# A two-layer decoder trunk on one core: eight-tile inversion on array quarters, S5's loads on another queue, eleven dummy products

## The chip, the cores and the metric

The kernel runs on one core of one Trainium2 chip. The metric is the device time of one execution in microseconds (us); the time before is the median of three runs. A profile is one execution recorded by the hardware profiler. TensorE is called PE, VectorE DVE, ScalarE ACT, GpSimd POOL, SyncE SP.

## What is computed

The reference is a decoder trunk of two layers over 1024 positions of width 1024, in float32. Layer 0 mixes positions by a gated DeltaNet (GDN, 8 heads of 128, chunks of 64 positions), layer 1 by a diagonal state-space model (S5, 64 groups of 16 channels). Beside each mixer runs a cross-attention into 256 memory tokens; an output projection, a layer norm, an MLP and another layer norm follow. Cut to what matters here:

```
a_strict = where(strict, einsum('bhnid,bhnjd->bhnij', kb, k) * decay, 0)
sol = triangular_solve(eye + a_strict, concat([vb, kb * exp(gc)]))    # per head and chunk
...                                                                   # scan over chunks with sol
st = sr + pr * h - pi * h ...                                         # S5: complex scan, chunk by chunk
y = Re(C st) + D u
x = LN(alpha * x + concat([mix, cross]) @ w_o);  x = LN(alpha * x + relu(x @ w1)**2 @ w2)
```

The kernel works in chunks of 128 positions, eight tiles a head, and inverts each tile's unit lower triangular 128x128 matrix (eye + a_strict) instead of solving with it.

## The kernel before, in words

**Large products.** The matrices of the projections and the MLP are split into a high and a low part of type fp32r, and three products replace one (`mm3`, lines 380 to 385; wi, wz, wu, q and so on in the profile). ACT makes the high part (L362, L851), DVE the low part (L363, L852). Small products (recurrence, inversion, S5's tables) are plain fp32, which PE runs as two instructions each.

**The GDN part.** For each head, `gdn_projections` makes keys, queries, values and the gate. `gdn_keys_out` writes the negated strictly lower matrices of a half (four tiles) to DRAM as ntf, and their diagonal blocks of 32 as ntd. `gdn_inverse_` inverts the blocks of 32 on DVE for two heads at a time and leaves them in DRAM as t32, once as they are and once transposed. `gdn_invert_tiles` then puts the blocks together: first from 32 to 64, then from 64 to the tile's 128. Before, this runs by halves of a head: four tiles at a time, five steps, each a few 128x128 products into the one bank of pool "pi" and copies out of it by ACT and DVE. Three constant tiles serve all heads: `bds[0]` and `bds[1]`, zeroed once, into which the blocks are loaded in diagonal position, and `zi`, which starts as identities and takes the lower left block of 32. The step that fills `zi` reads nm (from ntf) and bd; the following ones make iv in two forms (plain and transposed) and its lower left block. `gdn_fill` (L1405) weaves the steps into the projections of the head, at even distances (`each`). `gdn_recur` runs the recurrence over chunks, with the finished TT as stationary operand (pe, L1452), woven with the next head's projections.

**S5.** `s5_front` runs a fixed list of steps (FRONT): U projects the channels (wu, from the weight wur), D drives the scan of block m (p1 products with G, multiplication by the tables tab, the scan on DVE), R reads it (py products with M0 and H), K, Q, S, T and V are the memory attention. u goes out to DRAM (ud, L1978) and back in another layout (L2021); yd carries the result. G, H, tab and M0 are loads from DRAM that GpSimd issues, at lines 1983, 1997 and 2012. M0 lands in the same buffer for every m, so its load waits until the py products of the block before are through.

**The order of the work.** The kernel is written in a plain order, and then `settle` (from L58) reorders all engines' instructions of nearly the whole program. It prices each instruction (`price`), gives it a due time from PE's order, and simulates the engines: each takes, of what can start, what is due first; PE may take only what is due soon. DVE work named in `patient` (that of `gdn_inverse`) has its due time moved by 40 us. Among PE's products `kind` tells fp32r ("r") from fp32 ("f"), and a bonus keeps the same kind together. The order that comes out is pinned, engine by engine; each engine's queue runs strictly in that order, SP's and GpSimd's DMA issues too.

**The start.** `busy_start` issues eight products of ones on PE while the first inputs are loaded.

Of the kernel before, what the change touches and what calls it, by code (L numbers as in the profile page):

```python
# [10 lines left out]
F32 = mybir.dt.float32  # L11
F32R = mybir.dt.float32r
# [18 lines left out]
class Trunk:  # L31
# [26 lines left out]
    def settle(self, first, last, reach=0.0, ahead=15.0, passes=1, margin=0.0, late=0.0, hold=1e3, stay=(0.0, 0.0), turn_=0.0):  # L58
# [116 lines left out]
        lag = 0.05  # L175
        sets = [{AF.Exp: 0, AF.Tanh: 0, AF.Sin: 1, AF.Gelu_apprx_tanh: 2, AF.Sigmoid: 3}.get(i.func) if i.opcode == "Activation" else None for i in ins]
        turns = [x for x in range(n) if ins[x].engine == E.PE]
        best = None
        for _ in range(passes):
            due, now = [0.0] * n, 0.0  # L180
# [38 lines left out]
            while len(order) < n:  # L219
                first_ = None  # L220
                drift = free[E.PE] - due[turns[head]] if head < len(turns) else 0.0
                for e in names:
                    pick = None
                    for x in open_[e]:
                        if e == E.PE and x != turns[head] and due[x] > due[turns[head]] + reach - 1e-6:
                            continue
                        s = room(x) if fresh[x] else 0.0
                        if s is None:
                            continue
                        r = max(ready[x], s, free[e], due[x] - ahead if e != E.PE else 0.0)  # L230
                        if cost[x][2] > 1.5:
                            r = max(r, due[x] + drift - hold)
                        if e == E.PE and kind == "fr" and ins[x].ins[0].dtype == F32:
                            r += 0.15
                        other = 1.28 if sets[x] not in (None, table) else 0.0
                        if e == E.PE and kind and kind[-1] == "fr"[ins[x].ins[0].dtype == F32R]:
# [16 lines left out]
                    r = max(r, locked)  # L253
                    locked = r + busy
                if e == E.PE:
                    if kind[-1:] == "f" and ins[x].ins[0].dtype == F32R:
                        busy, length = busy + turn_, length + turn_
                    lost += r - free[e]
                    kind = (kind + "fr"[ins[x].ins[0].dtype == F32R])[-2:]
# [31 lines left out]
    def price(self, i, big):  # L291
# [602 lines left out]
    def gdn_consts(self):  # L894
# [17 lines left out]
        for o in self.bds:  # L912
            nc.gpsimd.memset(o, 0.0)
        self.zi = self.tile("h4", [P, 4, P], F32, "zi")
        nc.scalar.copy(self.zi, self.ident.unsqueeze(1).to_broadcast([P, 4, P]))
# [346 lines left out]
    def block_diag(self, h, hf, w):  # L1262

        o = self.bds[w]
        for b in (0, 2) if w == 0 else range(4):
            q = slice(32 * b, 32 * b + 32)
            to = o[q, :, q] if w == 0 else o[q, b // 2, :, 32 * (b % 2):32 * (b % 2) + 32]
            self.nc.sync.dma_start(to, self.t32[w, h, 4 * hf:4 * hf + 4, b].rearrange("t i c -> i t c"))
        return o

    def gdn_invert_tiles(self, h):


        nc = self.nc
        V = nc.vector
        first = lambda x: x.rearrange("p t (b k c) -> p t b k c", b=2, k=2)[:, :, :, 0, :]
        zi = self.zi
        bank = lambda: self.psum("pi", "iv", (P, 4, P))
        mm = lambda *a: nc.tensor.matmul(*a, start=True, stop=True)
        out = self.TT[h] = []  # L1280

        def pairs(left, right):
            ps = bank()
            for t in (0, 2):
                mm(ps[:, t // 2, :], left[:, t:t + 2].rearrange("p t c -> p (t c)"), right[:, t:t + 2])
            return [ps[64 * x:64 * x + 64, 0:2, 64 * x:64 * x + 64] for x in range(2)]

        for hf in range(2):
            nm = self.tile("h4", [P, 2, 4, 64], F32, "nm")
            for b in range(2):  # L1290
                nc.sync.dma_start(nm[:, 0, :, 32 * b:32 * b + 32], self.ntf[h, hf, :, :, 64 * b + 32:64 * b + 64])
            nc.sync.dma_start(nm[:, 1], self.ntf[h, hf, :, :, 64:128])
            T32, V32 = self.block_diag(h, hf, 0), self.block_diag(h, hf, 1)

            for x, q in enumerate(pairs(nm[:, 0], first(T32))):
                nc.scalar.copy(zi[32:64, x::2, 0:32], q[0:32, :, 0:32])
                V.tensor_copy(zi[96:128, x::2, 64:96], q[32:64, :, 32:64])
            yield 0.5

            o = self.tile("h4", [P, 4, 64], F32, "iv")  # L1300
            nc.gpsimd.memset(o[64:128], 0.0)
            for x, q in enumerate(pairs(V32[:, 0], zi[:, :, 0:64])):
                (nc.scalar.copy, V.tensor_copy)[x](o[0:64, x::2], q)
            yield 0.5

            TT = self.tile("h3", [P, 4, P], F32, "iv")
            ps = bank()
            for t in range(4):
                mm(ps[:, t, :], zi[:, t, :], V32[:, :, t, :])
            nc.scalar.copy(TT, ps)  # L1310
            yield 0.8
            for x, q in enumerate(pairs(nm[:, 1], o)):
                (nc.scalar.copy, V.tensor_copy)[x](o[64:128, x::2], q)
            yield 0.5
            for x, q in enumerate(pairs(o, TT[:, :, 64:128])):
                (nc.scalar.copy, V.tensor_copy)[x](TT[0:64, x::2, 64:128], q)
            out.append(TT)
            yield 0.5

    def gdn_queries_out(self, h, hf):  # L1320

# [658 lines left out]

    def s5_load(self, nm, tag, src):
        t = self.tile(tag, [P, 4, P], F32, nm)
        self.nc.gpsimd.dma_start(t, src)
        return t

    def s5_driving(self, m):

        out = []
        for b in range(2):
# [4 lines left out]
            for x in range(2):  # L1994
                t = self.tile("h2", [P, 4, P], F32, "tab")
                src = self.tabd[1:3, c, q] if x else self.tabd[0, c, q].unsqueeze(0).to_broadcast([2, 64, 4, P])
                self.nc.gpsimd.dma_start(t.rearrange("p g t -> p (g t)"), src.rearrange("k p g t -> k p (g t)"))
                tabs.append(t)
            out.append((G1, tabs))
        return out  # L2000
# [7 lines left out]
    def s5_local(self, m, o):  # L2008

        M0 = o.rearrange("p (g x) -> p g x", g=8)  # L2010
        z = self.zd[m]
        self.nc.gpsimd.dma_start(M0, bass.AP(z.tensor, z.offset, [[16, 8], [8 * 240, 16], [240, 8], [1, P]]))
        return M0

    def s5_drive(self, m, loads):
# [268 lines left out]
    def busy_start(self):  # L2284
# [4 lines left out]
        for o in ones:  # L2289
            nc.vector.memset(o, 1.0)  # L2290
        ps = self.psum("mm", "ws", (P, P))
        for n in range(8):
            o = ones[n > 0]
            nc.tensor.matmul(ps, o, o, start=True, stop=True)

# [167 lines left out]
```

## Time and profile before

| | before |
|---|---|
| median of three runs | 2501.77 us (2498.99 to 2503.67) |
| the profiled execution | 2499.32 us |
| its span, first to last instruction | 2497.3 us |
| mean granted clock of PE | 0.998 |
| PE, DVE, ACT, POOL busy | 2468.7, 1933.0, 1387.5, 275.4 us |
| DMA, share of 16 engines by queue | SP's 46.9%, GpSimd's 7.1%, ACT's 0.5% |

A line of the profile names the source line, the engine, the operation, what it writes and reads (buffer numbers left out) and how often. Durations on PE overlap, since matmuls are pipelined; so PE's pace is read from one start to the next. In the view of windows the columns are the busy time of PE, of its weight loads (PEld), of DVE, ACT and POOL, then the granted clock, the DMA share and GB/s.

### The profile page before, as it was taken

Reading aid. Unit: us, or ns where it says so; the run is one execution under the profiler, and the core shown is the slowest. Engines: PE = TensorE matmul, PEld = TensorE weight load, DVE = VectorE, ACT = ScalarE, POOL = GpSimd, SP = SyncE. Lnnn points to the kernel's source line nnn. Section 1 sums busy time; section 2 is a strip of 40 time slices with the busy share of each in tenths; the row PEclk is TensorE's granted clock in tenths of the full one; section 3 lists DMA queues with packets and bytes.
Section 4 is the critical chain, followed back from the end, with each engine's and each line's share of the span. In section 5 each row is a group of like instructions: output and inputs, shape, how many; then the busy total and the mean of one; then the engine's idle time right before and its main releaser. Section 6 shows DMA issues by size and latency. Waiting matters only on the chain. (4 is left out here: it accounts for less than half of the span.)

```text
span 2497.3 us, 36513 instructions
## 1 busy us (share of the span) xinstructions
PE 2468.7 (99%) x12199; PEld 2056.2 (82%) x12199; DVE 1933.0 (77%) x3661; ACT 1387.5 (56%) x3114; POOL 275.4 (11%) x405
## 2 busy tenths in 40 slices
PE   9999999999999999999999999999999999999998
PEld 7888888888787888888888888888887888888886
DVE  7776868676889987879988856683988655587777
ACT  7766677665557576554444254672466555544444
POOL 1111111110001011312120122200010000000001
PEclk9999999999999999999999999999999999999999
DMA  6445545566335665587455498884237544573422
GB/s 206 131 114 155 153 137 141 150 194 200 109 116 184 212 222 185 177 281 252 136 171 156 139 238 223 198 265 143 77 118 239 173 162 148 205 277 105 148 89 97
DMA packets 304844, 426.17 MB, mean 171 GB/s; under 512 B 132832, under 2 KB 150192, under 8 KB 304656
## 3 DMA queue, kind: packets, MB, share of 16 engines
q1 hardware_dynamic: 270320, 372.50, 46.9%
q0 software_dynamic: 31744, 46.76, 7.1%
q10 hardware_dynamic: 2592, 4.59, 0.5%
q8 instruction: 96, 1.57, 0.3%
q14 instruction: 92, 0.75, 0.1%
HBM read 287.84 MB, written 135.76 MB: 170 GB/s over the span
## 5 line engine op out<-in xcount | busy, mean ns | idle before, releaser
L383 PE MATMUL q<-wkh,hkh 128*128 128x512 f32 x784 | 305.9, 390 | 0.0
L384 PE MATMUL q<-wkl,hkh 128*128 128x512 f32 x784 | 305.7, 390 | 0.0
L385 PE MATMUL q<-wkh,hkl 128*128 128x512 f32 x784 | 305.4, 390 | 0.0
L851 ACT CAST wkh<-wr 128x512 fp32r<-128x512 f32 x168 | 104.8, 624 | 233.2 <-PE q L384 153.6
L383 PEld LDWEIGHTS q<-wkh,hkh 128*128 128x128 f32 x784 | 147.2, 188 | 31.7 <-ACT wkh L851 1.0
L385 PEld LDWEIGHTS q<-wkh,hkl 128*128 128x128 f32 x784 | 147.2, 188 | 30.3
L384 PEld LDWEIGHTS q<-wkl,hkh 128*128 128x128 f32 x784 | 147.2, 188 | 30.3
L852 DVE TENSOR_TENSOR wkl<-wr,wkh 128x512 fp32r<-128x512 f32 x168 | 115.6, 688 | 63.7 <-issue 50.2
L383 PE MATMUL wi<-xTh,wih 128*128 128x512 f32 x376 | 152.0, 404 | 0.0
L384 PE MATMUL wi<-xTl,wih 128*128 128x512 f32 x376 | 150.0, 399 | 0.0
L385 PE MATMUL wi<-xTh,wil 128*128 128x512 f32 x376 | 149.9, 399 | 0.0
L506 POOL TENSOR_TENSOR mv<-mv,mhalf 128x1 f32<-128x1 f32 x32 | 29.5, 922 | 981.0 <-DVE mv L500 936.3
L852 DVE TENSOR_TENSOR hkl<-hr,hkh 128x512 fp32r<-128x512 f32 x196 | 134.0, 684 | 3.3 <-ACT hkh L851 3.3
L851 ACT CAST hkh<-hr 128x512 fp32r<-128x512 f32 x196 | 120.8, 616 | 4.6 <-DMA hr<-hd 4.6
L383 PE MATMUL o<-ow,ok 128*128 128x512 f32 x256 | 101.3, 396 | 1.0 <-ACT ok L1714 1.0
L385 PE MATMUL o<-ow,ok 128*128 128x512 f32 x256 | 101.3, 396 | 0.2
L384 PE MATMUL o<-ow,ok 128*128 128x512 f32 x256 | 100.0, 390 | 0.0
L844 DVE TENSOR_TENSOR y<-q,y 128x512 f32<-128x512 f32 x136 | 88.0, 681 | 0.0
L385 PEld LDWEIGHTS wi<-xTh,wil 128*128 128x128 f32 x376 | 70.8, 188 | 12.7
L383 PEld LDWEIGHTS wi<-xTh,wih 128*128 128x128 f32 x376 | 70.9, 189 | 11.8
L384 PEld LDWEIGHTS wi<-xTl,wih 128*128 128x128 f32 x376 | 71.0, 189 | 11.6
L1714 ACT CAST ok<-os 128x512 fp32r<-128x512 f32 x56 | 34.7, 621 | 53.3 <-PE o L385 39.1
(621 smaller groups left out, 7335.0 us busy)
## 6 DMA issues: line engine op xcount, KB each, us to landing
hr<-hd SPq DMA_DIRECT2D x212, 256.0 KB, 2.8
wr<-in_w_dram SPq DMA_DIRECT2D x56, 512.0 KB, 4.8
hd<-u SPq DMA_DIRECT2D x100, 256.0 KB, 2.2
w1r<-in_w_dram SPq DMA_DIRECT2D x48, 512.0 KB, 3.7
hd<-hid SPq DMA_DIRECT2D x60, 256.0 KB, 2.3
hd<-p SPq DMA_DIRECT2D x60, 256.0 KB, 2.6
w1r<-in_w_dram SPq DMA_DIRECT2D x48, 256.0 KB, 3.4
wir<-in_w_in_dram SPq DMA_DIRECT2D x23, 512.0 KB, 4.8
```

Of the source, the lines that this page charges most:

```text
L383: mm(ps, a[0], b[0], start=start, stop=False, skip_group_check=onto)
L384: mm(ps, a[0], b[1], start=False, stop=False, skip_group_check=onto)
L385: mm(ps, a[1], b[0], start=False, stop=stop, skip_group_check=onto)
L506: nc.gpsimd.tensor_tensor(mv[:, 3:4], mv[:, 2:3], self.mhalf[:, 0:1], op=ALU.pow)
L844: V.tensor_tensor(o, bank[t], o, op=ALU.add)
L851: nc.scalar.copy(hi, s)
L852: nc.vector.tensor_tensor(lo, s, f32(hi), op=ALU.subtract)
L1714: nc.scalar.copy(hi, s)
```

## The change

The diff, cut to its core:

```diff
@@ settle
+        sort = ["r" if i.engine == E.PE and i.ins[0].dtype == F32R else
+                "n" if i.engine == E.PE and not i.is_transpose and i.outs[0].bass_ap.ap[0][1] < P else "f" for i in ins]
...
-                    due[x] += 40.0
+                    due[x] += 15.0
...
-                    if kind[-1:] == "f" and ins[x].ins[0].dtype == F32R:
+                    if kind[-1:] != "r" and sort[x] == "r":
                         busy, length = busy + turn_, length + turn_
+                    if kind and kind[-1] != sort[x] and "n" in (kind[-1], sort[x]):
+                        busy, length = busy + 0.14, length + 0.14
...
@@ price
-            return 0.01 + 1.66e-3 * wide * (part if part < 1 else 1), 0.39, 0
+            if part < 1:
+                return 0.01 + 1.66e-3 * max(wide, 64) * part, 0.35, 0
+            return 0.01 + 1.66e-3 * wide, 0.39, 0
@@ gdn_consts
-        self.bds = [self.tile("h4", shape, F32, "bd") for shape in ([P, 4, P], [P, 2, 4, 64])]
...
+        self.bd = self.tile("h4", [P, 8, 64], F32, "bd")
+        self.iv = self.tile("h4", [P, HALF], F32, "iv")
+        self.zi = self.tile("h4", [P, 8, 64], F32, "zi")
...
@@ gdn_invert_tiles
-        for hf in range(2):
-            nm = self.tile("h4", [P, 2, 4, 64], F32, "nm")
...
+        for hf in range(2):
             for b in range(2):
+                nc.sync.dma_start(n0[q[b], 4 * hf:4 * hf + 4], self.ntf[h, hf, q[b], :, 64 * b + 32:64 * b + 64])
+                nc.sync.dma_start(n1[q[b], 2 * hf:2 * hf + 2], self.ntf[h, hf, 0:64, b::2, 64:128])
+        for b in range(2):
+            nc.sync.dma_start(t32[64 * b:64 * b + 32], self.t32[0, h, :, 2 * b].rearrange("t i c -> i t c"))
+        for b in range(4):
+            k = 32 * (b % 2)
+            nc.sync.dma_start(bd[32 * b:32 * b + 32, :, k:k + 32], self.t32[1, h, :, b].rearrange("t i c -> i t c"))
+        ps = bank()
+        for j in range(4):
+            t = slice(2 * j, 2 * j + 2)
+            for b in range(2):
+                mm(ps[q[b], j], flat(n0[q[b], t]), flat(t32[q[b], t]))
...
+        ps, pt = bank(), self.psum("pa", "iv", (P, 8, 64))
+        for t in range(8):
+            mm(ps[q[t % 2], t // 2], bd[q[0], t], zi[q[0], t])
+        for t in range(8):
+            for b in range(2):
+                mm(pt[q[b], t], zi[q[b], t], bd[q[b], t])
...
+        ps, pt = bank(), self.psum("pa", "iv", (P, 8, 64))
+        for j in range(4):
+            for b, o in enumerate((ps, pt)):
+                mm(o[q[1], j], n1[q[b], j], v0[q[b], j])
...
+        ps = bank()
+        for t in range(8):
+            mm(ps[q[t % 2], t // 2], x[q[1], t], TT[t // 4][q[1], t % 4, q[1]])
...
@@ gdn_fill
-        each = (total - wait) / 10.5
+        each = (total - wait) / 4.5
@@ s5_load, s5_driving, s5_local (the same in each)
-        self.nc.gpsimd.dma_start(t, src)
+        self.nc.sync.dma_start(t, src)
@@ busy_start
-        for n in range(8):
+        for n in range(11):
```

So the inversion now handles all eight tiles of a head at once, in four steps. Every product is 64 by 64 by 64: its operands lie in one half of the partitions (the rows of the array), its result in one half of the partitions of a bank (the columns). In step one (8 products) and the second part of step two (16) the halves of rows and columns go together, and neighbours alternate between the two. In the first part of step two (8) and in step four (8) all products use the same half of the rows and alternate between the columns; in step three (8) they alternate between the rows, write the same columns, and do so in two banks. `settle` and `price` know the new sort of product ("n"), and its order is computed anew for the whole program.

Three places show it. First PE, in the projections of a head (wz the gate, iv the inversion, qt and qk the queries). Before:

```order
L383 MATMUL wz_6667<-xTh_17_142,wzh_6663 128x512
L384 MATMUL wz_6667<-xTl_18_143,wzh_6663 128x512
L1279 MATMUL iv_6321<-bd_104,zi_107 128x128 x4
L385 MATMUL wz_6667<-xTh_17_142,wzl_6664 128x512
L383 MATMUL wz_6667<-xTh_17_142,wzh_6663 128x512
L384 MATMUL wz_6667<-xTl_18_143,wzh_6663 128x512
L385 MATMUL wz_6667<-xTh_17_142,wzl_6664 128x512
L1279 MATMUL iv_6338<-iv_6303,nm_6277 128x128 x2
```

PE at the same kind of place in the changed kernel:

```order
L390 MATMUL wz_3534<-xTl_18_147,wzh_3530 128x512
L391 MATMUL wz_3534<-xTh_17_146,wzl_3531 128x512
L1279 MATMUL iv_3415<-zi_108,bd_106 64x64 x8
L1279 MATMUL iv_3416<-bd_106,zi_108 64x64 x16
L1347 MATMUL qt_3493<-ident,qT_3090 128x128 x4
L1362 MATMUL qk_3509<-qT_3090,kT_323 128x128 x4
L1279 MATMUL iv_3515<-iv_107,nm_3312 64x64
L1279 MATMUL iv_3516<-iv_107,nm_3312 64x64
```

Before, two or four products of the inversion stand alone between others, 84 such groups over the program; now step two's 24 stand together and step three follows after eight others, and there are 36 groups.

Second, SP in the middle of S5, before (ud and s5t<-ud are u's way out and back, wur the weights of U, yd the result):

```order
L1978 DMA ud<-s5t_14779 128x8x128
L353 DMA wur_15556<-in_w_in_dram 128x1024
L2063 DMA yd<-zg_15404 128x512
L2063 DMA yd<-zg_15416 128x512
L2021 DMA s5t_14779<-ud 128x1024
L353 DMA wur_15762<-in_w_in_dram 128x1024
```

and on GpSimd at the same time, before (s5t<-zd is M0):

```order
L2012 DMA s5t_14779<-zd 128x8x128
L1983 DMA G_2944_15464<-g1d 128x512
L1983 DMA G_2947_15470<-g1d 128x512
L1983 DMA H_2950_15477<-h1d 128x4x128
L1983 DMA H_2951_15479<-h1d 128x4x128
```

Third, SP at this place in the changed kernel:

```order
L1997 DMA ud<-s5t_14839 128x8x128
L359 DMA wur_15616<-in_w_in_dram 128x1024
L2082 DMA yd<-zg_15464 128x512
L2031 DMA s5t_14839<-zd 128x8x128
L2082 DMA yd<-zg_15476 128x512
L2002 DMA G_2896_15524<-g1d 128x512
L2002 DMA G_2899_15530<-g1d 128x512
L2002 DMA H_2902_15537<-h1d 128x4x128
L2002 DMA H_2903_15539<-h1d 128x4x128
L2040 DMA s5t_14839<-ud 128x1024
L359 DMA wur_15822<-in_w_in_dram 128x1024
```

M0, G and H now stand between a block's first weight and the next one, ahead of u's way back. The tables tab moved to SP in the same way.

More of the change, by code (lines that the diff above doesn't have):

```diff
@@ L232, in settle @@
                             r = max(r, due[x] + drift - hold)
-                        if e == E.PE and kind == "fr" and ins[x].ins[0].dtype == F32:
+                        if e == E.PE and kind[-1:] == "r" and kind != "rr" and sort[x] != "r":
                             r += 0.15
                         other = 1.28 if sets[x] not in (None, table) else 0.0
-                        if e == E.PE and kind and kind[-1] == "fr"[ins[x].ins[0].dtype == F32R]:
+                        if e == E.PE and kind and kind[-1] == sort[x]:
                             other -= stay[ins[x].name in self.grouped]
@@ L910, in gdn_consts @@
         self.early = [early[:, 2 * P + 64 * n:2 * P + 64 * (n + 1)].rearrange("p (t h) -> p t h", t=8) for n in range(2)]
-        self.bds = [self.tile("h4", shape, F32, "bd") for shape in ([P, 4, P], [P, 2, 4, 64])]
[L912 to L915, printed above, removed]
+        self.bd = self.tile("h4", [P, 8, 64], F32, "bd")
+        self.iv = self.tile("h4", [P, HALF], F32, "iv")
+        self.zi = self.tile("h4", [P, 8, 64], F32, "zi")
+        nc.gpsimd.memset(self.bd, 0.0)
+        nc.gpsimd.memset(self.iv, 0.0)
+        for b in range(2):
+            q = slice(64 * b, 64 * b + 64)
+            nc.scalar.copy(self.zi[q], self.ident[q, q].unsqueeze(1).to_broadcast([64, 8, 64]))
         cw = scr[:, P + 8 + 13 * 64:].rearrange("p (m j) -> p m j", j=4)
@@ L1260, in gdn_inverse_ @@
             nc.gpsimd.dma_start(dst[0][:, 16:32, 8 * y:8 * y + 8], Tn[q])
[L1262 to L1269, printed above, removed]
     def gdn_invert_tiles(self, h):
@@ L1275, in gdn_invert_tiles @@
         V = nc.vector
-        first = lambda x: x.rearrange("p t (b k c) -> p t b k c", b=2, k=2)[:, :, :, 0, :]
-        zi = self.zi
-        bank = lambda: self.psum("pi", "iv", (P, 4, P))
+        zi, bd = self.zi, self.bd
+        q = [slice(64 * b, 64 * b + 64) for b in range(2)]
+        bank = lambda: self.psum("pi", "iv", (P, 8, 64))
         mm = lambda *a: nc.tensor.matmul(*a, start=True, stop=True)
[L1280 to L1286, printed above, removed]
+        flat = lambda x: x.rearrange("p t c -> p (t c)")
@@ L1288, in gdn_invert_tiles @@
+        copy = (nc.scalar.copy, V.tensor_copy)
+        nm = self.tile("h4", [P, HALF], F32, "nm")
+        n0 = nm[:, 0:256].rearrange("p (t c) -> p t c", t=8)
+        n1 = nm[:, 256:512].rearrange("p (j c) -> p j c", j=4)
+        t32 = self.iv[:, 0:256].rearrange("p (t c) -> p t c", t=8)
+        v0 = self.iv[:, 256:512].rearrange("p (j c) -> p j c", j=4)
         for hf in range(2):
-            nm = self.tile("h4", [P, 2, 4, 64], F32, "nm")
             for b in range(2):
-                nc.sync.dma_start(nm[:, 0, :, 32 * b:32 * b + 32], self.ntf[h, hf, :, :, 64 * b + 32:64 * b + 64])
@@ L1292, in gdn_invert_tiles @@
[L1292 to L1316, printed above, removed]
@@ L1317, in gdn_invert_tiles @@
-            out.append(TT)
-            yield 0.5
+                nc.sync.dma_start(n0[q[b], 4 * hf:4 * hf + 4], self.ntf[h, hf, q[b], :, 64 * b + 32:64 * b + 64])
[5 more added lines that the diff above has]
+            nc.sync.dma_start(bd[32 * b:32 * b + 32, :, k:k + 32], self.t32[1, h, :, b].rearrange("t i c -> i t c"))
@@ new lines, in gdn_invert_tiles @@
+        ps = bank()
[3 more added lines that the diff above has]
+                mm(ps[q[b], j], flat(n0[q[b], t]), flat(t32[q[b], t]))
+        for b in range(2):
+            for e in range(2):
+                r = 64 * b + 32 * e
+                copy[e](zi[64 * b + 32:64 * b + 64, e::2, 0:32], ps[r:r + 32, 0:4, 32 * e:32 * e + 32])
+        yield 0.8
+        ps, pt = bank(), self.psum("pa", "iv", (P, 8, 64))
+        for t in range(8):
+            mm(ps[q[t % 2], t // 2], bd[q[0], t], zi[q[0], t])
@@ new lines, in gdn_invert_tiles @@
+        for t in range(8):
+            for b in range(2):
+                mm(pt[q[b], t], zi[q[b], t], bd[q[b], t])
+        TT = self.TT[h] = [self.tile("h3", [P, 4, P], F32, "iv") for _ in range(2)]
+        V.tensor_copy(v0, ps[:, 0:4])
+        for hf in range(2):
+            nc.gpsimd.memset(TT[hf][q[1], :, q[0]], 0.0)
+            for b in range(2):
+                nc.scalar.copy(TT[hf][q[b], :, q[b]], pt[q[b], 4 * hf:4 * hf + 4])
+        yield 1.7
+        ps, pt = bank(), self.psum("pa", "iv", (P, 8, 64))
@@ new lines, in gdn_invert_tiles @@
+        for j in range(4):
+            for b, o in enumerate((ps, pt)):
+                mm(o[q[1], j], n1[q[b], j], v0[q[b], j])
+        x = self.tile("h4", [P, 8, 64], F32, "x2")
+        for b, o in enumerate((ps, pt)):
+            copy[b](x[q[1], b::2], o[q[1], 0:4])
+        yield 0.8
+        ps = bank()
+        for t in range(8):
+            mm(ps[q[t % 2], t // 2], x[q[1], t], TT[t // 4][q[1], t % 4, q[1]])
+        for hf in range(2):
+            for b in range(2):
+                copy[b](TT[hf][q[0], b::2, q[1]], ps[q[b], 2 * hf:2 * hf + 2])
@@ L1320, in gdn_queries_out @@
+        yield 0.8
     def gdn_queries_out(self, h, hf):
@@ L1996, in s5_driving @@
                 src = self.tabd[1:3, c, q] if x else self.tabd[0, c, q].unsqueeze(0).to_broadcast([2, 64, 4, P])
-                self.nc.gpsimd.dma_start(t.rearrange("p g t -> p (g t)"), src.rearrange("k p g t -> k p (g t)"))
+                self.nc.sync.dma_start(t.rearrange("p g t -> p (g t)"), src.rearrange("k p g t -> k p (g t)"))
                 tabs.append(t)
@@ L2011, in s5_local @@
         z = self.zd[m]
-        self.nc.gpsimd.dma_start(M0, bass.AP(z.tensor, z.offset, [[16, 8], [8 * 240, 16], [240, 8], [1, P]]))
+        self.nc.sync.dma_start(M0, bass.AP(z.tensor, z.offset, [[16, 8], [8 * 240, 16], [240, 8], [1, P]]))
         return M0
```

2 lines of the change are left out of this document (1 added, 1 removed).

## The prediction

> **What bounds the kernel now.** I read the page first: which engine fills the span.
>
> ```profile
> span 2497.3 us, 36513 instructions
> PE 2468.7 (99%) x12199; PEld 2056.2 (82%) x12199; DVE 1933.0 (77%) x3661; ACT 1387.5 (56%) x3114; POOL 275.4 (11%) x405
> ```
>
> TensorE (PE) is busy for all but 28.6 us, so only two things shorten the kernel: fewer PE microseconds, or fewer PE waits. The waits of PE come next (total, times, longest), then two windows: the heads of the GDN layer and the S5 mixer.
>
> ```profile
> PE iv L1279 <- issue: 1.8, 3, 1.5
> PE wu L383 <- ACT wuh L362: 1.4, 1, 1.4
> PE iv L1279 <- DVE iv L1313: 1.3, 1, 1.3
> PE pv L383 <- ACT pTh L1592: 1.1, 2, 0.9
> ...
> 100.00:650.00 550.00, 544.97 (x3107) 467.06 (x3106) 399.49 (x815) 369.08 (x1166) 78.72 (x110) 1.00 0.55 157
> 1400.00:1650.00 250.00, 245.09 (x1378) 211.76 (x1377) 167.24 (x317) 130.19 (x229) 57.27 (x73) 0.99 0.83 217
> ```
>
> No wait is large. The two groups the change touches, the tile inversion (iv, L1279) and S5's weights (wu), lead the list with 3.1 and 1.4 us. The last column but one is the DMA share: 0.55 among the heads, 0.83 in S5. DVE and ACT have room in both.
>
> **Part 1, the inversion's products.** The tile view of iv counts what goes: a product in fp32 is two instructions, so these 384 are 192 products, 24 a head.
>
> ```profile
> L1279 PE MATMUL iv<-bd,zi x128: 270/275/377, 180.6 to 628.2; 128*128 128x128 f32 x128
> L1279 PE MATMUL iv<-bd,nm x64: 270/275/377, 174.8 to 618.3; 128*128 128x128 f32 x64
> L1279 PE MATMUL iv<-zi,bd x64: 270/275/348, 178.1 to 626.2; 128*128 128x128 f32 x64
> L1279 PE MATMUL iv<-iv,nm x64: 270/275/348, 184.2 to 631.5; 128*128 128x128 f32 x64
> L1279 PE MATMUL iv<-iv,iv x64: 270/275/377, 186.9 to 633.8; 128*128 128x128 f32 x64
> ```
>
> Durations overlap, so the price is read from start to next start, in PE's timeline:
>
> ```profile
> 627.40 1.05 PE L1279 MATMUL iv<-bd,zi 128*128 128x128 f32 x8
> 628.29 0.39 PE L1458 MATMUL pS<-e,kdl 128*128 128x128 f32 x2
> ```
>
> Eight instructions, four products, take 0.89 us: 0.2225 each, and 192 of them 42.7 us, all on the path.
>
> In their place stand 48 products of 64x64 by 64 a head, 384 in all, each on a quarter of the array. No such product runs before; the nearest row is S5's pz (L1949), whose eight products lie on four strips of 32 columns:
>
> ```profile
> L1949 PE MATMUL pz<-H,co x128: 272/273/297, 1001.2 to 1303.3; 128*32 128x128 f32 x128
> ...
> 1000.65 0.39 PE L384 MATMUL pC<-xB,s1h 128*128 128x512 f32 x1
> 1000.88 0.39 PE L385 MATMUL pC<-xB,s1l 128*128 128x512 f32 x1
> 1001.20 0.64 PE L1949 MATMUL pz<-H,co 128*32 128x128 f32 x16
> 1001.77 0.50 PE L383 MATMUL pA<-xB,a2h 128*128 128x512 f32 x1
> 1002.11 0.40 PE L384 MATMUL pA<-xB,a2h 128*128 128x512 f32 x1
> ```
>
> Sixteen instructions of 273 ns end within 0.64 us: the last starts 0.37 after the first, so strips overlap. Between the starts 1000.88 and 1002.11 lie two full products of 0.23 (1000.65 to 1000.88) and the group: 1.23 - 0.46 = 0.77 us. If a round on four strips takes as long as one product on the whole array, a pz product costs 0.2225/4 = 0.056, eight 0.45, and going into the strips and out again the other 0.32. A new product streams half as many columns with half as many neighbours beside it: again 0.056, with 0.050 (0.37/15 per instruction) as its lower end and 0.111 (half of 0.2225, nothing overlapping) as its upper. The built order holds 36 unbroken groups of them, 4 to 5 a head. Sum: 384 x 0.056 + 36 x 0.32 = 21.5 + 11.5 = 33.0 us against 42.7, so -9.7 us. The ends are -12.0 (0.050) and +11.5 (0.111).
>
> The Trainium skill (TensorE: Matmul & The Clock Gate, section "What overlaps and what doesn't") says that weight loads overlap running products only where the row group differs. The pz strips all use the same rows and overlap nevertheless, so by the trace the rule doesn't hold for column strips; what it would make of the sum is the second rival below.
>
> **The chain between the products.** A half of a head went through five dependent steps, ten a head; now there are four a head. The visible waits before L1279 are 3.1 us (1.8 + 1.3). Three of the four steps have other products between them, and where a step follows at once (after the 24 of step two) sixteen products cover the copy. I take 2.0 of the 3.1 as gained, 0 to 3.1 as the range. The weights moved by the smaller patience (15 for 40) change which DVE work goes first; DVE is at 399 of 550 us in this window, so I put that at nothing; without that room it would show as waits of kk or iv.
>
> **Part 2, S5's loads on SP's queue.** The window holds one event that costs more than its wait. In order: SP's issue of a weight, ACT's cast, PE, then the windows (clock is the last column but two), and the DMA view of 1488 to 1512 (median us to landing).
>
> ```profile
> 1493.39 0.33 SPq L353 DMA_DIRECT2D wur<-in_w_in_dram  x1
> 1505.17 1.04 ACT L362 CAST wuh<-wur 128x1024 fp32r<-128x1024 f32 x1 [6.50 <-DMA wur<-in_w_in_dram]
> 1506.27 0.50 PE L383 MATMUL wu<-xTh,wuh 128*128 128x512 f32 x1 [1.43 <-ACT wuh L362]
> 1507.53 0.75 PE L385 MATMUL wu<-xTh,wul 128*128 128x512 f32 x1 [0.52 <-DVE wul L363]
> 1500.00:1510.00 10.00, 8.05 (x30) 5.96 (x29) 4.61 (x10) 2.75 (x4) 1.20 (x2) 0.88 0.96 333
> 1510.00:1520.00 10.00, 10.00 (x44) 8.19 (x44) 4.29 (x7) 2.69 (x6) 2.04 (x3) 0.95 0.41 111
> wur<-in_w_in_dram SPq DMA_DIRECT2D x2, 512.0 KB, 8.8
> G<-g1d POOLq DMA_DIRECT2D x2, 256.0 KB, 11.4
> H<-h1d POOLq DMA_DIRECT2D x2, 256.0 KB, 12.3
> q1 hardware_dynamic: 2045, 3.66, 51.1%
> q0 software_dynamic: 2237, 2.38, 39.9%
> ```
>
> The weight took 11.8 us to ACT while GpSimd's queue (q0) held 39.9% of the DMA engines for the M0, G and H loads. PE idled 1.43 + 0.52, and then the granted clock was 0.88 and 0.95 over ten microseconds each: 1.2 + 0.5 = 1.7 us. Together 3.7 us. In the new order the same weight stands ahead of the M0, G and H loads on one queue, so it doesn't share with them: I take -3.7, one stall and its clock loss. Issuing is no burden: SP takes 0.33 us a load. But a wait that GpSimd bore is now SP's (the total over six times, and the longest):
>
> ```profile
> POOL s5t L2012 <- PE py L2060: 56.4, 6, 12.1
> ```
>
> Behind that wait on SP now stand yd, G, H, the u of the next block and the weight after it; drive waits for G and u, ACT's cast for the weight. The lower bound of this part is -6 (the pv wait and smaller ones go too), the upper +22 (rival four).
>
> **Part 3, eleven dummies.**
>
> ```profile
> 1.71 3.19 PE L2294 MATMUL ws<-ws 128*128 128x128 f32 x14
> 6.23 0.49 PE L974 MATMUL wi<-xTl,wih 128*128 128x512 f32 x1
> 7.59 0.50 PE L974 MATMUL wi<-xTh,wih 128*128 128x512 f32 x1 [0.87 <-ACT xTh L957]
> ```
>
> Fourteen take 3.19 us, so six more end about 1.3 later, near 6 us. The first two real products slip; the third ends before 7.59, where PE waits for ACT anyway. Nothing; without that cover 0.5 us.
>
> **The sum.** -9.7 - 2.0 - 3.7 = -15.4 us. The profiled execution took 2499.32, 2.45 under the median 2501.77 of three; taken from the median, 2486.4. Every engine's order is computed anew, though, and the waits outside the two parts (28.6 - 3.1 - 2.0 = 23.5 us of PE) fall elsewhere: +-6.
>
> **Rivals.**
> 1. The quarters do not overlap: 0.111 a product gives +11.5 for -9.7, 2507.6, slower. For it: no row shows row quarters side by side. Against: pz. It decides at 0.081 a product, where the products alone cost as before. Chance 0.08.
> 2. Only products on different rows overlap. Step two's first eight and step four's eight (128 in all) share their rows: 128 x (0.111 - 0.056) = +7.0, 2493.4. Against it pz, which shares all rows. Chance 0.10. It is the skill's rule above.
> 3. Different rows may not write one bank of PSUM at once. Step one and the sixteen of step two (192 products) do so, on different partitions: +10.6, 2497.0. No trace row shows it either way. Chance 0.12. The Trainium skill states such a rule (TensorEngine Tiling (Array Packing), section "Gotcha 1: PSUM Pressure").
> 4. SP waits for py and the weights behind it come late. The margin was already used up once (11.8 us from issue to cast), and the wait is up to 12.1. If each of the six later weights stalls PE as the one seen, 6 x 3.7 = +22.2 for -3.7: 2512.3, slower. It decides when a weight reaches ACT later than its first product's turn. Chance 0.08.
> 5. The inversion's PE time comes back as waits of the recurrence on ACT and DVE, and the S5 stall moves: no change, 2501. Against it: PE always had projections to run, 544.97 of 550. Chance 0.10.
>
> **How the numbers follow.** The forecast has 0.52, the rivals 0.48. 0.2% of the median, 5.0 us, is about what a measurement can tell: faster is below 2496.8, slower above 2506.8. Faster: 0.52 + 0.10 + 0.04 (a third of rival 3, which lies on the edge) = 0.66. Same: 0.08 + 0.10 = 0.18. Slower: 0.08 + 0.08 = 0.16. Range: the low end has 0.050 a product (-2.3), all waits (-1.1), S5's -6 (-2.3) and the new order's -6: 2474.7, so 2474. The high end takes in rivals 2, 3 and 5 with some of the order's +6, and leaves out rivals 1 and 4: 2503.
>
> **What would show it.** L1279's 768 instructions should start about 28 ns apart inside a group, with some 0.3 us lost around it; 56 ns would be rival 1, 56 ns in steps two (first eight) and four alone rival 2, in one and two (sixteen) rival 3. No clock below 1.00 from 1400 to 1650, and wu's waits gone; waits of wu, p or py there would be rival 4. The forecast is wrong if PE's busy time falls by 10 us and its waits grow as much.

## The result, and the profile after

| | before | after |
|---|---|---|
| median of five runs each | 2500.97 us (2498.55 to 2503.67) | 2583.04 us (2579.36 to 2586.81) |
| ratio, 95% interval | | 1.033 [1.0315, 1.0345] |
| the profiled execution | 2499.32 us | 2586.81 us |
| its span | 2497.3 us | 2585.1 us |
| mean granted clock of PE | 0.998 | 0.981 |

The kernel became 82 us slower, where 15 us faster was forecast. Two executions of the runs below, one of `e13_patience0` (3073.11 us) and one of the kernel before beside `e10_sums_first` and `e11_old_inversion` (6416.69 us), were far slower than all others and are left out of the ratios and ranges. The page of the changed kernel first: span and engines, the slices of PE's clock (two of them, over S5, are below 9), and GpSimd's queue.

```profile
span 2585.1 us, 37071 instructions
PE 2480.4 (96%) x12589; PEld 2054.5 (79%) x12589; DVE 1929.5 (75%) x3629; ACT 1382.7 (53%) x3091; POOL 225.7 (9%) x333
...
PEclk9999999999999999999999799899999999999999
...
q0 software_dynamic: 10112, 25.64, 3.2%
```

PE was busy for all but 28.6 us before; now it is for all but 104.7. PE's waits of the changed kernel (total, times, longest) name the place:

```profile
PE wu L389 <- ACT xTh L540: 31.5, 1, 31.5
PE wq L389 <- ACT wqh L368: 10.5, 1, 10.5
PE wu L389 <- ACT wuh L368: 9.8, 1, 9.8
PE py L2079 <- DMA H<-h1d: 9.7, 4, 2.6
PE py L2078 <- DMA s5t<-zd: 7.6, 3, 4.4
```

All five are S5. The tile views of wu and py (min/median/max ns, then the first and last start in us) give its length, first for before, then for after:

```profile
L383 PE MATMUL wu<-xTh,wuh x128: 389/389/628, 1416.8 to 1594.6; 128*128 128x512 f32 x128
...
L2060 PE MATMUL py<-r,H x128: 274/274/275, 1467.0 to 1640.0; 128*128 128x127 f32 x128
```

```profile
L389 PE MATMUL wu<-xTh,wuh x128: 389/389/796, 1418.0 to 1663.3; 128*128 128x512 f32 x128
...
L2079 PE MATMUL py<-r,H x128: 274/275/581, 1501.3 to 1726.1; 128*128 128x127 f32 x128
```

From the first wu to the last py: 1640.0 - 1416.8 = 223.2 us before, 1726.1 - 1418.0 = 308.1 after: 84.9 of the 87.8 us between the two spans. Windows over this stretch (columns as before), first of the kernel before, then of the changed one, show what it is made of: the same 1239 instructions of PE, 68.9 us more of idle time (73.8 for 4.9) and 16.0 us more of busy time, with a mean clock of 0.87 for 0.99. The DMA engines are half empty (0.51 for 0.87). The last two lines are the changed kernel's long wait; in its middle the clock is 0.50:

```profile
1416.80:1640.30 223.50, 218.59 (x1239) 189.68 (x1238) 142.96 (x271) 118.55 (x205) 51.21 (x65) 0.99 0.87 222
1418.00:1726.40 308.40, 234.57 (x1239) 200.37 (x1238) 143.12 (x271) 118.69 (x205) 0.55 (x1) 0.87 0.51 160
1430.00:1440.00 10.00, 0.78 (x8) 0.54 (x5) 0.00 (x0) 0.00 (x0) 0.00 (x0) 0.71 0.13 51
1440.00:1460.00 20.00, 0.00 (x0) 0.00 (x0) 0.00 (x0) 0.00 (x0) 0.00 (x0) 0.50 0.42 152
```

The longest wait can be followed back. PE waits for xTh, which ACT makes; on ACT, in order, a cast of mem stands ahead and waits 34.33 us for its load; on SP that load (of 1448.72) stands behind eight loads of tab. ACT's and then SP's timeline of the changed kernel:

```profile
1460.10 1.14 ACT L1529 CAST memh<-mem 128x512 fp32r<-128x512 f32 x2 [34.33 <-DMA mem<-in_memT_dram]
1461.14 0.58 ACT L1991 COPY s5t<-wu 128x512 f32<-128x512 f32 x1
1461.62 1.07 ACT L540 CAST xTh<-xt 128x512 fp32r<-128x512 f32 x2
```

```profile
1412.34 31.27 SPq L2016 DMA_DIRECT2D tab<-tabd  x8
1443.70 4.92 SPq L2002 DMA_DIRECT2D G<-g1d  x1
1448.72 0.46 SPq L359 DMA_DIRECT2D mem<-in_memT_dram  x1
```

Eight issues occupy SP for 31.27 us, the first two for 0.5 each and the other six for 3.4 to 7.1; the ninth, of G, whose load spreads over 128 partitions, is held for 4.92 right behind them. The tile views of tab, before and after, show how long one issue took (min/median/max ns):

```profile
L1997 POOL DMA_DIRECT2D tab<-tabd x32: 787/816/866, 1367.9 to 1585.2; - x32
```

```profile
L2016 SPq DMA_DIRECT2D tab<-tabd x32: 485/2937/7113, 1369.0 to 1668.8; - x32
```

The DMA view of the changed kernel from 1415 to 1440 us, where almost nothing but tables moves (packets, MB, share of 16 engines):

```profile
DMA packets 611, 1.25 MB, mean 50 GB/s; under 512 B 8, under 2 KB 8, under 8 KB 610
...
q1 hardware_dynamic: 610, 1.23, 13.1%
```

13.1% of 16 is 2.1 engines, at 50 GB/s: a load of 256 KB takes some 5.2 us, so eight take 42. In the code (L2016) the outermost dimension of the load's pattern, on both sides, is k = 2: one table broadcast twice, or two tables. **Theory A**: such a load on SP's queue is carried by two engines; SP, once the queue is full, is held at its next issue; and what stands behind (mem, y, weights, u) comes late. **Theory B** (rival four of the prediction): SP stands waiting for py at M0's load. **Theory C**: the newly computed order, with the changed inversion, does it.

The inversion itself did what was forecast. PE's timeline of the changed kernel: step two's 48 instructions, a group of step three and one of step four, each with what follows.

```profile
598.17 0.62 PE L1279 MATMUL iv<-zi,bd 64*64 64x64 f32 x13
598.58 0.27 PE L1279 MATMUL iv<-bd,zi 64*64 64x64 f32 x1
598.58 0.28 PE L1279 MATMUL iv<-zi,bd 64*64 64x64 f32 x3
598.68 1.10 PE L1279 MATMUL iv<-bd,zi 64*64 64x64 f32 x31
599.71 0.49 PE L1477 MATMUL pS<-e,kdl 128*128 128x128 f32 x2
...
608.30 0.68 PE L1279 MATMUL iv<-iv,nm 64*64 64x64 f32 x16
608.92 0.49 PE L1465 MATMUL ks<-S,kT 128*128 128x128 f32 x2
...
623.77 0.68 PE L1279 MATMUL iv<-iv,x 64*64 64x64 f32 x16
624.38 0.49 PE L1465 MATMUL ks<-S,kT 128*128 128x128 f32 x2
```

48 instructions take 1.54 us, 32 ns each with the way in and out; the groups of 16 take 0.62 and 0.61. Summed from every start of L1279 to the next start of any product, the inversion takes 31.2 us where it took 41.8: 10.5 us less (9.7 forecast). Yet the first output projection (o), right behind the heads, starts at 632.6 for 634.2, only 1.6 us earlier (one execution each).

### The profile page after: what moved, and what is told of

It reads as the page before. It is cut to its first block, busy times and chain, and to the rows that moved or that the text cites. A ratio compares the mean times of both kernels' runs of the same rounds, so it can differ in the third digit from the quotient of the medians.

```text
span 2585.1 us, 37071 instructions
## 1 busy us (share of the span) xinstructions
PE 2480.4 (96%) x12589; PEld 2054.5 (79%) x12589; DVE 1929.5 (75%) x3629; ACT 1382.7 (53%) x3091; POOL 225.7 (9%) x333
## 5 line engine op out<-in xcount | busy, mean ns | idle before, releaser
L857 ACT CAST wkh<-wr 128x512 fp32r<-128x512 f32 x168 | 104.7, 623 | 237.0 <-PE q L390 155.3
L390 PEld LDWEIGHTS q<-wkl,hkh 128*128 128x128 f32 x784 | 147.2, 188 | 30.1
L389 PE MATMUL wu<-xTh,wuh 128*128 128x512 f32 x128 | 52.2, 408 | 41.2 <-ACT xTh L540 31.5
L390 PEld LDWEIGHTS wi<-xTl,wih 128*128 128x128 f32 x376 | 71.6, 190 | 12.6
```

Of the source, the lines that this page charges most:

```text
L389: mm(ps, a[0], b[0], start=start, stop=False, skip_group_check=onto)
L390: mm(ps, a[0], b[1], start=False, stop=False, skip_group_check=onto)
L857: nc.scalar.copy(hi, s)
```

## The experiments

Each ratio is to the kernel before, run on the same chip.

**Undo or repair the tables alone.** Four kernels, three from the changed one and one from the kernel before.

`e1_split`, the changed kernel with each load of tab as two of 64 partitions:

```diff
-                self.nc.sync.dma_start(t.rearrange("p g t -> p (g t)"), src.rearrange("k p g t -> k p (g t)"))
+                for k in range(2):
+                    self.nc.sync.dma_start(t[64 * k:64 * k + 64], self.tabd[k + 1 if x else 0, c, q])
```

> The changed kernel with each load of a table tab (2 blocks of 64 partitions in one DMA) issued as two DMAs of 64 partitions each, all still on SP's queue. Theory A (a tab load whose outermost dimension is 2 uses two DMA engines on SP's queue, some 5 us each, and the in-order queue behind it waits): S5 goes back to the length it had before the change, total about 2495 us. Rival B (SP stands waiting for py at M0's load, and the weights behind it come late): no change, about 2583. Rival C (the new order of all engines is bad in S5): over 2560, since the order is computed from the same prices.

Measured 2494.01 us (2492.32 to 2494.73), ratio 0.9972 [0.996, 0.9983]. SP's timeline of this kernel at the same place:

```profile
1409.61 7.23 SPq L2016 DMA_DIRECT2D tab<-tabd  x10
1416.93 0.54 SPq L2002 DMA_DIRECT2D G<-g1d  x1
1417.52 1.73 SPq L2016 DMA_DIRECT2D tab<-tabd  x3
1419.36 0.52 SPq L359 DMA_DIRECT2D mem<-in_memT_dram  x1
```

The same bytes in twice as many issues, and mem is issued at 1419.36 instead of 1448.72; G's issue takes 0.54 us instead of 4.92, so what held it was the queue, not its own load. The loss is gone and the kernel beats both.

`e2_tab_pool`, the changed kernel with tab's loads alone back on GpSimd:

```diff
-                self.nc.sync.dma_start(t.rearrange("p g t -> p (g t)"), src.rearrange("k p g t -> k p (g t)"))
+                self.nc.gpsimd.dma_start(t.rearrange("p g t -> p (g t)"), src.rearrange("k p g t -> k p (g t)"))
```

> The changed kernel with the loads of tab alone back on GpSimd; G, H and M0 stay on SP. Theory A: about 2495 us, nothing of the 82 us is left. Rival B (M0's wait on SP): about 2583, since M0 still stands there. Rival C: anything between.

Measured 2494.89 us (2491.54 to 2496.94), ratio 0.9977 [0.9966, 0.9987]. G, H and M0 stay on SP, so theory B falls here.

`e3_all_pool`, the changed kernel with tab, G, H and M0 all back on GpSimd (the same replacement at L2002, L2016 and L2031): the inversion, the order and the dummies alone.

> The changed kernel with all of S5's loads back on GpSimd, so the inversion, its order and the dummies alone. Theory A: the 82 us are gone; the heads give the 1.6 us by which the output projection starts earlier in the changed kernel's trace, so about 2499 us, same as before. The prediction's own sum for this part (-9.7 and -2.0) would give about 2489.

Measured 2499.1 us (2495.3 to 2503.7), ratio 0.9995 [0.9986, 1.0004]: no loss, so theory C falls, but no gain either. PE's order was not the matter: in `e1_split`, `e3_all_pool` and `e9_split_columns` its 12589 instructions run in the order of the changed kernel, one for one by name and shape.

`e4_tab_only_sp`, the kernel before with tab's loads alone (L1997) moved from `gpsimd` to `sync`.

> The kernel before with only the loads of tab moved to SP's queue. Theory A: the whole loss, 2575 to 2590 us. Rival B (M0's wait on SP, which isn't moved here): about 2500.

Measured 2596.74 us (2593.43 to 2599.98), ratio 1.0383 [1.0369, 1.0398]. One edited line makes the whole loss and more.

**Is it the outermost dimension, or the size and number of the loads?** `e9_split_columns`, the changed kernel with each load of tab cut in two along the columns, so that each half still has k = 2 outermost:

```diff
+                for g in range(2):
+                    s = src[:, :, 2 * g:2 * g + 2]
+                    self.nc.sync.dma_start(t[:, 2 * g:2 * g + 2].rearrange("p g t -> p (g t)"), s.rearrange("k p g t -> k p (g t)"))
```

> The changed kernel with each load of tab issued as two that take half of the columns each, on all 128 partitions, so that each is still two by 64 rows, of 1 KB. Theory A (a load whose outermost dimension is two is carried by two DMA engines): still slow, 2570 to 2600, with the wait of the first wu product for xTh above 20 us. Rival G (the split into two smaller loads, or more loads under way at once, is what made the split kernel fast): 2494, within 3.

Measured 2582.68 us (2581.95 and 2583.4), ratio 1.0321 [1.0303, 1.0339], and its longest wait is the same:

```profile
PE wu L389 <- ACT xTh L540: 25.2, 1, 25.2
```

As many loads as in the fast kernel, of the same 128 KB, and as slow as the changed one: it is the pattern's outermost dimension. From 1415 to 1433 us, while only tables move, the DMA rate is 48 GB/s, against 50 in the changed kernel. Rival G falls.

**S5's loads without the tables.** `e6_rest_only_sp`, the kernel before with `gpsimd` replaced by `sync` at L1983 (G, H) and L2012 (M0) only.

> The kernel before with G, H and M0 alone loaded by SP; the tables stay with GpSimd, the inversion is the old one. Theory A (the S5 term of the forecast, -3.7 us, is real, and only the tables' loads spoil it): 2496.8, between 2494 and 2499, and no clock below 1.00 between 1400 and 1650 us. Rival D (the gain of the split tables' kernel in S5 comes from its newly computed order, not from the loads' queue): 2500.5, within 1.5 of the kernel before. Rival B (SP waits for py and weights come late): slower than before.

Measured 2498.43 us (2494.82 to 2501.45), ratio 0.9982 [0.9974, 0.9991], 4.5 us. From the first wu to the last py it takes 1638.5 - 1418.8 = 219.7 us, 3.5 less than before; 1500 to 1510 us, where the clock had been 0.88, now reads:

```profile
1500.00:1510.00 10.00, 9.19 (x41) 7.30 (x40) 9.63 (x19) 4.02 (x7) 2.29 (x3) 1.00 0.98 317
```

With the tables split on SP as well (`e1_split`) S5 takes 1633.9 - 1415.2 = 218.7.

**The dummies.** `e8_dummies8`, `e1_split` with `range(8)` for `range(11)`.

> The changed kernel with each load of tab issued as two of 64 partitions, and with eight dummy products instead of eleven. By the forecast (the dummies cost and bring nothing): 2494.0 within 1.5. A rival (the full clock comes earlier with eleven, after 4.0 us for 5.7): up to 1.8 us slower, 2495.8.

Measured 2495.11 us (2491.43 to 2496.57), ratio 0.9969 [0.9956, 0.9981], against 0.9972 with eleven: nothing.

**Where the inversion's gain went.** Windows over the last pair of heads, kernel before and then `e1_split`:

```profile
540.00:560.00 20.00, 20.00 (x118) 17.35 (x117) 18.42 (x33) 11.04 (x37) 0.00 (x0) 1.00 0.52 150
560.00:580.00 20.00, 20.00 (x113) 17.33 (x112) 15.34 (x29) 12.00 (x33) 4.08 (x5) 1.00 0.51 154
```

```profile
540.00:560.00 20.00, 20.00 (x113) 17.14 (x112) 19.84 (x35) 9.46 (x33) 1.64 (x3) 1.00 0.24 76
560.00:580.00 20.00, 16.71 (x138) 12.63 (x138) 10.39 (x20) 8.99 (x23) 3.11 (x4) 0.83 0.77 225
```

PE loses 3.3 us idle here and 3.4 us of clock (0.17 x 20). It waits for wi, whose weight SP issues at 560.36 us; that weight's buffer was held by w1r, whose sums (L631 to L634) stood on DVE behind the inverses of 32, while DVE was busy for 19.84 of 20 us. **Theory E**: the smaller patience did that.

`e7_patience40`: `e1_split` with `due[x] += 40.0` for 15.

> The changed kernel with each load of tab issued as two of 64 partitions, and with the old patience of 40 us for the small inverses on DVE. Theory E (the smaller patience puts the inverses of two heads ahead of the sums over w1 on DVE just before 560 us, the sums hold the buffer of a weight, that weight comes late, and PE loses its clock; this is where the inversion's gain goes): the late wi product near 567 us and the clock below 1.00 there vanish, and the time falls by 4 to 7 us from the 2494.0 of the same kernel with patience 15, to 2487 to 2490. Rival F (the gain is lost to waits of the recurrence wherever they fall): with the patience back, other waits of iv, ks and pe grow, and the time stays at 2492 to 2496 or rises.

Measured 2509.07 us (2507.89 to 2511.06), ratio 1.0028 [1.0017, 1.0039], against 0.9972 with the smaller patience. Its first wait is new:

```profile
PE iv L1279 <- DMA iv<-t: 10.1, 3, 6.5
```

Step one of eight tiles needs the inverses of 32 of the whole head at once, and with the old patience they come late three times. Theory E falls in this form: the smaller patience is needed.

`e13_patience0`: the same with `+= 0.0`.

> The changed kernel with each load of tab issued as two of 64 partitions, and with patience 0: the inverses of 32 have no handicap on DVE. Theory H (DVE's inverses come too late for the first step of a pair): the first step's wait goes and the time falls to 2488 to 2491. Rival I (other DVE work for the projections and the recurrence is displaced by as much): 2493 to 2498, with waits of ks, pe or wi in place of iv.

Measured 2507.39 us (2504.0 to 2510.8), ratio 1.002 [1.0008, 1.0031]. The waits of iv are nearly gone (0.2 us), as theory H said, but the time rises. Now waits of kk, pS, ks and qt lead among the heads: other DVE and ACT work is late. Rival I's mechanism, at a higher price than it gave; 15 lies between two losses.

`e10_sums_first`: `e1_split`, and in `settle` the four sums over w1 due 20 us earlier:

```diff
+                if ins[x].name in self.eager and ins[x].engine == E.DVE:
+                    due[x] -= 20.0
```

> The changed kernel with each load of tab issued as two of 64 partitions, patience 15, and the four sums over w1 (and only these DVE instructions) due 20 us earlier, so that they stand ahead of the last inverses on DVE. Theory E in its second form (what costs the inversion its gain is that these sums, which hold the weight's buffer, come behind the inverses and the weight behind them comes late; the patience itself is right for eight tiles): the wait of wi for ACT near 567 us and the clock below 1.00 from 560 to 580 vanish, and the time falls by 5 to 7 us, from 2494 to 2487 to 2489. Rival F (the gain is lost to waits wherever they fall): 2492 to 2496.

Measured 2492.01 us (2491.0 to 2496.63), ratio 0.997 [0.9961, 0.998]: no gain that can be told from `e1_split`, so theory E falls in its second form too. The wait for wih is gone, as expected, but its windows show another loss in its place, 3.7 us idle and a clock of 0.81:

```profile
560.00:580.00 20.00, 16.28 (x118) 13.20 (x117) 9.68 (x19) 5.75 (x13) 3.06 (x4) 0.81 0.61 165
580.00:600.00 20.00, 19.55 (x178) 16.15 (x177) 12.18 (x24) 11.76 (x42) 2.14 (x3) 0.94 0.33 80
```

PE's timeline of this kernel there: the recurrence's chain, then half pace, then the inversion's own chain.

```profile
563.23 0.49 PE L1476 MATMUL pe<-R,iv 128*128 128x128 f32 x2 [0.82 <-DVE R L1472]
564.07 0.49 PE L1482 MATMUL pS<-e,kdl 128*128 128x128 f32 x2 [0.35 <-ACT e L1478]
...
576.22 0.97 PE L1284 MATMUL iv<-zi,bd 64*64 64x64 f32 x13 [2.31 <-issue]
```

`e11_old_inversion`: its counterpart with the old inversion, patience 40 and eight dummies; S5's loads as in `e1_split`, the sums early too.

> The kernel before, with its old inversion by halves, patience 40 and eight dummies, and with all of S5's loads on SP, each load of tab as two of 64 partitions, and the same sums over w1 due 20 us earlier. It is the kernel of the run beside it without the new inversion. Theory E: the old inversion had no late weight near 560 us, so the earlier sums bring nothing here, and only S5's loads count: 2496 to 2498; the run beside it is then 8 to 10 us faster, about what the inversion's products save. Rival F: both within 3 us of each other.

Measured 2496.4 us (2495.16 to 2497.28), ratio 0.9988 [0.9979, 0.9996]. The early sums bring nothing here, as expected; but `e10_sums_first` is only 0.18% better (4.4 us), not 8 to 10 us. This pair, run on one chip, shows most directly what the new inversion is worth with its patience.

`e12_later_steps`: `e10_sums_first` with the steps of every other head begun later:

```diff
-            fill = self.gdn_fill(h + 1, xT, 22.0 if h % 2 else 0.0)
+            fill = self.gdn_fill(h + 1, xT, 22.0 if h % 2 else 12.0)
```

> The kernel of the earlier sums (split tables, patience 15, sums over w1 due 20 us earlier), and the inversion's four steps of heads 2, 4 and 6 begun 12 us later in the projections of the head. Theory H (PE, 10 us shorter, comes to the first step of a pair of heads before DVE has its inverses of 32 ready; with the steps later, other products stand before it): the waits and the low clock between 560 and 600 us fall by more than half, and the time is 2486 to 2489 against 2492.0. Rival I (the head is short of any other PE work there, so that the steps' own chain of copies and loads, or the recurrence behind it, is exposed wherever it stands): 2491 to 2497.

The edit does not do what was expected of it. It fills head h + 1, so the 12.0 goes to heads 1, 3, 5 and 7; heads 2, 4 and 6, whose first step opens a pair of heads, keep their 22.0. The traces agree. Head 3's first step, in `e10_sums_first` and then here:

```profile
333.01 0.68 PE L1284 MATMUL iv<-iv,nm 64*64 64x64 f32 x16
347.31 0.68 PE L1284 MATMUL iv<-iv,nm 64*64 64x64 f32 x16
```

The first steps of heads 2 and 4 stay (306.7 and 438.0 us for 306.9 and 437.6), that of head 6 comes 4.1 us earlier (568.5 for 572.6).

Measured 2490.76 us (2487.87 to 2493.88), ratio 0.9953 [0.9936, 0.9969], the fastest of all, and between the ranges of theory H and rival I. The windows from 540 us on:

```profile
540.00:560.00 20.00, 20.00 (x113) 17.01 (x112) 20.00 (x36) 10.76 (x34) 2.12 (x4) 1.00 0.48 169
560.00:580.00 20.00, 18.04 (x176) 14.88 (x176) 10.43 (x23) 11.21 (x36) 2.17 (x3) 1.00 0.67 170
580.00:600.00 20.00, 20.00 (x151) 17.22 (x151) 15.96 (x30) 11.45 (x36) 1.62 (x3) 1.00 0.52 158
```

No low clock, 2.0 us idle, and o starts at 623.9 us: 10.3 earlier than before, so in this execution most of the saving reaches the end of the heads. Theory H is not tested by this, since the steps it names did not move later. What differs between the two traces is what PE has to run: from 561.7 to 565.0 us `e10_sums_first` has only the recurrence's products, with waits between them, until the low part of a weight (wil) comes from DVE; here products of wz and wi run without a gap until 571.0. Why moving the odd heads' steps does this stays open. How much it is worth on the median is unsure too: the profiled execution of `e10_sums_first` was the slowest of its ten, the two ratios differ by 0.17% (4 us), and their intervals just overlap.

## Why the prediction was wrong

**The step that failed** is in part 2: "Issuing is no burden: SP takes 0.33 us a load." The row behind it is a weight's load, whose outermost dimension is the 128 partitions. The loads that moved include 32 of tab, with an outermost dimension of two, which the diff shows. On SP their issue took 2.9 us (median) and up to 7.1, and everything behind them on the queue came late: mem's load went out 36.4 us after the first of the eight (1448.72 - 1412.34), for 9.8 with the tables split (1419.36 - 1409.61). No row of before shows such a load on SP; that called for bounds, as the inversion's products got them, and the +22 of rival four was the bound of another mechanism. This one line is worth +96 us by itself (`e4_tab_only_sp`, 2596.74 against 2500.44).

The Trainium skill has a rule that bears on this (DMA: Bandwidth & Descriptors, section "Why a DMA increments its semaphore by 16 and not by 1"): the number of DMA engines is the largest up to 16 that divides the slowest dimension of both sides, SP's queue always takes the lowest-numbered ones, and GpSimd's takes successive ones in turn. The 2.1 engines on SP's queue agree with its first half. That rule, weighed against the tab lines of the diff, would have made a rival that ends on the slow side.

**S5's stall, -3.7 us: right, without the tables.** `e6_rest_only_sp` has 3.5 us less in S5 and 4.5 on the ratio, and the clock of 0.88 is gone.

**The inversion's products, -9.7: mechanism and size right.** 10.5 us less in the changed kernel, and 12.5 less in `e12_later_steps` (29.2 for 41.8). Both terms were a little high: a group of 48 instructions takes 1.54 us for a forecast 48 x 0.028 + 0.32 = 1.66, a group of 16 takes 0.61 for 0.77; so was the old products' price, 42.7 us for the 41.8 summed. Rival two would have given about 1.2 us to a group of 16 in step four, which took 0.61; rival three the same pace of 56 ns to step two's last 32, which ran at 33. Rival one falls with them.

**The chain between the products, -2.0, and patience at nothing: wrong.** The heads ended 1.6 us earlier instead of 11.7, in `e1_split` 3.5. Rival five, given 0.10, describes it: the saved PE time came back as waits, with the clock lost behind them, most of them between 560 and 580 us. Its counter-argument, that PE always had projections to run, fails there: from 562.2 to 567.4 us in `e1_split` PE has only the recurrence's products. The prediction's cover, DVE "at 399 of 550 us", is a mean; in the 20 us before the loss DVE is full (19.84). That alone doesn't decide it, though: DVE is as full there in `e12_later_steps` (20.00), which loses no clock, and less so in `e10_sums_first` (18.28), which does. The smaller patience moved the first step of a pair of heads, to 307, 438 and 569 us in `e1_split` from 324, 457 and 582 before; with eight tiles at once and the old patience (`e7_patience40`) they stand at 320.5, 457.8 and 588.5, and PE waits for the inverses. Both a larger and a smaller patience cost more. So the term that failed, and where the time went, are shown; what makes PE run short of other products near 560 us even with the weight in time (`e10_sums_first`), and why later steps of the odd heads mended it in the trace, stays open.

**The dummies, 0: right** (`e8_dummies8`).

**Rival four** had the right queue and victims (weights and mem late behind S5's loads), but a wrong cause and a quarter of the price. SP did not stand waiting for py: with G, H and M0 on SP and tab off it (`e2_tab_pool`), the kernel is faster than before.

## What to carry to other kernels

Before a load is moved to another queue, look at the outermost dimension of its access pattern, not at another load's issue time: if it is small (2 here; M0's load, with 8 outermost in DRAM, moved without loss in `e6_rest_only_sp`), split the load along it into loads of many partitions (or leave it where it is). On a queue that runs in order, price the move by everything behind it, here a cast's load, ACT's queue and PE. And where a step is made shorter by doing more at once, ask when the last of its inputs is ready and what other work fills the stretch until then (in `e7_patience40` PE waited 10.1 us for them). When an experiment shifts some steps, check in the trace which ones moved.

## What the hardware showed that was not expected

The same loads of tab do no such harm on GpSimd's queue. In `e2_tab_pool` from 1415 to 1440 us, with the tables still moving:

```profile
q1 hardware_dynamic: 2009, 3.98, 56.0%
q0 software_dynamic: 2508, 1.61, 30.1%
```

30.1% of 16 is 4.8 engines for GpSimd's queue, against 2.1 on SP's; the rule above of the Trainium skill (DMA: Bandwidth & Descriptors, section "Why a DMA increments its semaphore by 16 and not by 1"), by which GpSimd's queue takes its engines in turn, would explain it, but no run shows which engines were used. The loads are not quick there either: in `e2_tab_pool` one takes 12.6 us (median) from issue to landing, in `e1_split`, split on SP, 5.8. But GpSimd's issues take 0.79 us each and are not held, and mem, the weights and u no longer stand behind them. Which of these makes them harmless no run separates. Products of 64x64 on quarters of the array, in fp32, went at about 33 ns an instruction, whether neighbours shared their rows or wrote one bank from different rows.
